# Hybrid decoder trunk on one core: gating chains of the SSD mixer apart and longer, banks of transposed attention weights held longer, the queries' second copy on GpSimd, three longer delays

## The chip, the core and the metric

The kernel runs on one core of a Trainium2 chip. The core has a matrix engine (TensorE, PE in the profile, with its weight loads as PEld), a vector engine (VectorE, DVE), an activation engine (ScalarE, ACT), a general engine (GpSimd, POOL) and a queue that issues most transfers (SyncE, SP). The metric is the device time of one execution in microseconds (us). The kernel before took 1032.54 us (median of 3 runs, 1031.77 to 1033.56).

## The reference

Two layers, each with one RMSNorm, one shared input projection, four parallel mixers and one shared output projection; then a last RMSNorm. Sequence 512, width 1024, all in fp32.

```python
for l in range(DEPTH):                                   # DEPTH = 2
    u = rmsnorm(h, norm_w[l])
    proj = einsum('bsd,de->bse', u, w_in[l])
    ret_p, diff_p, ssd_p, ml_p = split_cols(proj, ...)
    ret_out  = retention_mixer(rq, rk, rv, cos, sin) * silu(rz)
    diff_out = diff_attention_mixer(dq, dk, dv, lam, lam_init, ...) * silu(dz)
    y = ssd_mixer(xbc, dt_raw, ...)
    ssd_out  = _rms(y * silu(sz)) * ssd_norm_w[l]        # one rms over all 512 columns
    ml_out   = mlstm_mixer(mqk, mv, mo, mg, ...) * silu(mz)
    mix = concatenate([ret_out, diff_out, ssd_out, ml_out])
    h = h + einsum('bse,ed->bsd', mix, w_out[l])
return rmsnorm(h, final_norm_w)
```

Differential attention, per block of 128 queries and per head, subtracts two softmaxes:

```python
s = einsum('bqhtd,bkhtd->bhtqk', qi, k)                  # t = 0, 1: two score maps
p = softmax(where(mask, s, NEG_INF))
a = p[:, :, 0] - lam * p[:, :, 1]
out = einsum('bhqk,bkhe->bqhe', a, v)                    # then _rms and norm_w
```

## The kernel before

**Precision.** Each fp32 product is made of three matmuls: weights and activations are split into a high part (cast to fp32r, `whi`, `uh`, `mh`) and the rest (`wlo`, `ul`, `ml`), and hi*hi, hi*lo and lo*hi are summed in one bank. A weight piece comes by a transfer into a buffer `raw` (two of them, 128 x 1024 each, line 370), ACT casts its halves to `whi` (L361), DVE subtracts to get `wlo` (L362); ten buffers of each.

**Tiling.** The 512 positions are four blocks t of 128; a projection of 512 columns is a tile `pspj` of one bank of the matrix engine's accumulator, 24 matmuls of 128x512. There are eight banks. `psum` takes a bank off a heap ordered by the time at which it was put back, `free(p, lag)` puts it back with the modelled time plus `lag`. So `lag` does not wait for anything; it decides which bank the next tile takes. The real wait is a semaphore: the first matmul into a bank waits for the last read of what was there before.

**Order.** Only TensorE's order is written by hand. A planner runs the program in Python with a modelled TensorE clock `clk`. `filler` yields one projection after another in the order of the table `ORDER` (mLSTM's parts, then attention's dk, dq, dv, dz, output projection m, SSD's xs, bc, output projection d, rqk, sz, rv, rz, s, r); each of the four mixers is a generator that is put in by `spawn` and says by `yield x` how many us of matmuls are to stand before its next step. The table `W` has these delays: `dQ` from the split of a head's queries to its scores, `sB` from an SSD chunk's scores to its output, `mB3` the same in mLSTM's last chunk, `sF` from the reduction of a gated SSD chunk to the 128x1 matmul that sums its squares. Other engines' orders follow from the order of issue and a scheduler's priorities; each engine runs its own list in order.

**Places that the change touches.**
- `fin_s` (L1048 to 1076), once per SSD chunk t, after `silu(sz)` is there: gate on GpSimd (L1057), squares and cast on ACT, `ml` on DVE (L1063), the reduction of the squares on DVE into a buffer `bt` (L1065; two buffers), then a delay `sF`, a matmul 128x1 with ones, `m` on DVE (L1070), the power -0.5 on GpSimd. All four chains begin at the same time, when the last `sz` is there.
- `split_q` (L1158 to 1168), once per head: ACT copies each half of 64 rows of the queries to its own rows (L1164) and to the other rows (L1167), DVE makes the low part `ql` (L1165).
- `diff` (L1185 on): scores `psS` into two banks, mask, maximum and exponential (L1206 to 1208, high priority), mix of the two maps (L1215). `diff_av` (L1222 to 1240): transposes of the weights into a bank (L130), its copy to `w` on DVE (L1231, even t) or ACT (L1229, odd t), then the products with v into `psacc`.
- `layer`: in layer 0 the parameters' set-up `params2` is spawned after the first projection.

Of the kernel before, what the change touches and what calls it, by code (L numbers as in the profile page):

```python
# [56 lines left out]
END = {"cv", "cvh", "nlam", "aneg", "fac"}  # L57


W = {'norm': 9.0, 'g1': 1.5, 'g2': 7.3, 'g3': 1.8, 'g4': 12.4, 'mB': 1.8, 'mB3': 3.0, 'mC': 1.3, 'mN': 5.0, 'mF': 9.6, 'sB': 10.2,  # L60
     'sN': 0.0, 'sF': 6.0, 'rC': 2.3, 'rN': 3.0, 'dT': 9.14, 'dN': 1.0, 'dM': 3.0, 'dV': 6.68, 'dF': 14.0,
     'm0': 6.4, 's0': 8.8, 'dT1': 0.6, 'dN1': 1.0, 'he': 100, 'hr': 50, 'hd': 50, 'dS': 4.7, 'dQ': 6.0,
     'ha': 50}


# [31 lines left out]
class Trunk:  # L97
# [228 lines left out]
    def norm_in_t(self, t):  # L326
# [5 lines left out]
        for half in range(2):  # L332
# [3 lines left out]
            us.append(u)  # L336
        yield W["norm"]
        for half in range(2):
# [276 lines left out]
    def ev_conv(self, dst, which, f0, last=None):  # L615
        nc = self.nc

        def f(j, p):
            w = self.cvh[:, which, f0 + j, :]
            acc = self.ev()  # L620
            with self.tc.high_priority(W["he"]):
                if j == last:
# [14 lines left out]
    def ev_rope(self, sink, scale=1.0):  # L637
# [3 lines left out]
        def f(j, p):  # L641
            x = self.ev()
            with self.tc.high_priority(W["hr"]):
                for q in range(4):
# [73 lines left out]
    def gates(self):  # L718
# [11 lines left out]
        self.free(p)  # L730
        yield W["g1"]
        pt = self.psum()
# [22 lines left out]
        for i in range(7, 0, -1):  # L755
# [7 lines left out]
                                op=ALU.mult)  # L763
        yield W["g2"]
        pc = self.psum()
# [28 lines left out]
        nc.vector.tensor_copy(out=st[:, :, 64:68], in_=tot[:, :, 8:12])  # L794
        yield W["g3"]
        pr = self.psum()
# [253 lines left out]
    def fin_s(self, t, y, zs, res, l, fac):  # L1050


        nc = self.nc
        yield from self.pause(("sz", l, 3))
        for j in range(4):
            js = slice(j * P, (j + 1) * P)
            nc.gpsimd.tensor_tensor(out=y[:, js], in0=y[:, js], in1=zs[j][:, t * P:(t + 1) * P], op=ALU.mult)  # L1057
        sq = self.ev()
        nc.scalar.activation(sq, y, AF.Square)
        mh = self.t("mh", [P, 512], F32R, bufs=4)  # L1060
        ml = self.t("ml", [P, 512], F32R, bufs=4)
        nc.scalar.copy(out=mh, in_=y)
        nc.vector.tensor_tensor(out=ml, in0=y, in1=mh.bitcast(F32), op=ALU.subtract)  # L1063
        s = self.t("bt", [P, 256], bufs=2)
        nc.vector.tensor_reduce(out=s[:, 0:P], in_=sq.rearrange("p (j t) -> p t j", j=4), axis=AX.X, op=ALU.add)  # L1065
        yield W["sF"]
        p = self.psum()
        self.mm(p[:, 0:1], lhsT=s[:, 0:P], rhs=self.ones[:, 0:1])
        m = self.sm([P, 1])
        nc.vector.tensor_scalar(m, p[:, 0:1], 0.25 / GW, EPS, ALU.mult, ALU.add)  # L1070
        self.free(p)
        self.rsqrt(fac[:, t:t + 1], m, 1)
        res.append((mh, ml))
        self.done.add(("s", l, t))
# [83 lines left out]
    def split_q(self, x):  # L1158

        nc = self.nc  # L1160
        hi = [self.t("qs", [P, 512], F32R, bufs=2) for _ in range(2)]
        for j in range(2):
            own, oth = slice(j * 64, j * 64 + 64), slice(64 - j * 64, 128 - j * 64)
            nc.scalar.copy(out=hi[j][own, :], in_=x[own, :])  # L1164
            nc.vector.tensor_tensor(out=self.ql[j][own, :], in0=x[own, :], in1=hi[j][own, :].bitcast(F32),  # L1165
                                    op=ALU.subtract)
            nc.scalar.copy(out=hi[j][oth, :], in_=x[own, :])  # L1167
        return hi

    def split_k(self, dst):  # L1170
# [51 lines left out]
    def diff_av(self, l, t, h, a, o, v):  # L1222
        nc = self.nc
        n = (t + 1) * P
        pa = self.tr4([a[:, j * P:(j + 1) * P] for j in range(t + 1)])
        at = self.pg()
        with self.tc.high_priority(W["ha"]):
            if t % 2:
                nc.scalar.copy(out=at[:, 0:n], in_=pa[:, 0:n])  # L1229
            else:  # L1230
                nc.vector.tensor_copy(out=at[:, 0:n], in_=pa[:, 0:n])  # L1231
        self.free(pa)
        yield W["dV"]
        yield from self.pause(("dv", l, t))
        hs = slice(h * P, (h + 1) * P)
        for j in range(t + 1):
            self.mm(o[:, t * P:n], lhsT=at[:, j * P:(j + 1) * P], rhs=v[j][:, hs], start=(j == 0), stop=(j == t))
        self.done.add(("av", l, t, h))
# [43 lines left out]
    def layer(self, l, last):  # L1282

        nc = self.nc
        mv, th, mq, mk, mz, rm = [], [], [], [], [], []
        dv, dz, dq, dk, rd = [], [], [], [], []
        xs, bc, sz, rs = [], [], [], []
        qk, rv, rz, rr = [], [], [], []
        first = [True]
        fac = self.sm([P, NT], tag="fac", bufs=2)  # L1290

        def begin():
            if l:
                yield from self.proj_tok("mv", self.ev_vaug(mv))
            else:
                yield from self.start(self.ev_vaug(mv))
                self.spawn(self.params2(0))

        def mixer(gen, delay=0.0):
            def f():  # L1300
                self.spawn(gen(), delay)
                return ()
            return f

        def got_q(h, x):
            dq.append(x)
            self.done.add(("dq", l, h))

        def after(t):
            if last:  # L1310
                return self.final_t(t)
            if first[0]:
                first[0] = False
                self.params(l + 1)
                self.norm_in()
            return self.norm_in_t(t)

        def end():
            if last:
                self.load_nw(DEPTH, nc.scalar)  # L1320
            yield from self.out_proj("r", rr, True, after, last)

        tok = lambda name, evac: lambda: self.proj_tok(name, evac)
        feat = lambda name, evac: lambda: self.proj_feat(name, evac)
        return {

            "mv": begin,
            "gates": mixer(self.gates),
            "mq": feat("mq", self.ev_conv(mq, 1, 0)),
            "mk": feat("mk", self.ev_conv(mk, 1, 4)),  # L1330
            "mlstm": mixer(lambda: self.mlstm(mv, th, mz, mq, mk, rm), W["m0"]),
            "mo": tok("mo", self.ev_tanh(th)),
            "mz": tok("mz", self.ev_silu(mz, "z", 8)),
            "m": lambda: self.out_proj("m", rm),

            "dk": feat("dk", self.ev_rope(self.split_k(dk))),
            "dv": tok("dv", self.ev_v(dv)),
            "diff": mixer(lambda: self.diff(dq, dk, dv, dz, rd), W["dS"]),
            "dq": feat("dq", self.ev_rope(got_q, 0.125)),
            "dz": tok("dz", self.ev_silu(dz, "z", 8)),  # L1340
            "d": lambda: self.out_proj("d", rd, heads=True),

            "xs": feat("xs", self.ev_conv(xs, 0, 0)),
            "bc": feat("bc", self.ev_conv(bc, 0, 4, 3)),
            "ssd": mixer(lambda: self.ssd(xs, bc[0:2], bc[2:4], sz, rs, fac), W["s0"]),
            "sz": feat("sz", self.silu_feat(sz)),
            "s": lambda: self.out_proj("s", rs, fac=fac),

            "rqk": feat("rqk", self.ev_rope(lambda j, x: qk.append(x))),
            "rv": tok("rv", self.ev_v(rv)),  # L1350
            "ret": mixer(lambda: self.retention(qk, rv, rz, rr)),
            "rz": tok("rz", self.ev_silu(rz, "z", 8)),
            "r": end,
        }
# [77 lines left out]
```

## Time and profile before

| what | value |
|---|---|
| median of 3 runs | 1032.54 us (1031.77 to 1033.56) |
| the profiled execution | 1032.78 us |
| its span, first to last instruction | 1030.9 us, TensorE's mean granted clock 0.995 |
| TensorE busy | 1010.3 us, 98% of the span |
| VectorE, ScalarE, GpSimd busy | 704.4 us (68%), 496.2 us (48%), 170.0 us (16%) |
| chain that ended last, by engine | PE 86%, DVE 6%, DMA 4%, issue 2%, ACT 1% |

TensorE is busy nearly all the time, so what it does not do for want of data is read from the waits of that engine: the view of waits sums the idle time before its instructions by what ended it. A time line lists instructions with start and duration; where an instruction was late, the idle time and its releaser stand in brackets. Rows with the same line and form that follow one another are put together (x4).

### The profile page before, as it was taken

To read this page: it belongs to the slowest core of one execution; us is meant where nothing else is said; L and a number is where in the kernel's file an instruction comes from. 1 tells how busy PE (TensorE), PEld (TensorE's weight loads), DVE (VectorE), ACT (ScalarE), POOL (GpSimd) and SP (SyncE) were. 2 spreads that over 40 slices of the span, in tenths; PEclk is the share of its full clock that TensorE was granted. 3 is DMA by queue.
4 is the path that set the end of the run, shared out by engine and by line. 5 is a ranking of instruction groups with operands and counts; after the bars stand their busy time and mean duration, and the time that the engine had idled before them with its cause. 6 is when DMAs were issued, how large, how long until landed. Compare 5 with 4: busy or idle time off the path is not lost.

```text
span 1030.9 us, 14248 instructions
## 1 busy us (share of the span) xinstructions
PE 1010.3 (98%) x5096; PEld 831.6 (81%) x5096; DVE 704.4 (68%) x1532; ACT 496.2 (48%) x1077; POOL 170.0 (16%) x227
## 2 busy tenths in 40 slices
PE   9999999999999999899999999999999999989997
PEld 6788888788888887778887888887888888878786
DVE  5587676568887866446555967667687787863464
ACT  5445337656565344324353443576564553643332
POOL 1000132201111143122000012211011102421301
PEclk9999999999999999999999999999999999999999
DMA  7333322222212333214122432323141233242112
GB/s 257 109 89 107 103 72 86 85 95 82 82 51 93 106 86 102 75 63 128 42 82 83 132 94 73 92 82 103 62 123 42 82 100 105 86 119 82 41 62 82
DMA packets 39145, 93.84 MB, mean 91 GB/s; under 512 B 3849, under 2 KB 16777, under 8 KB 38946
## 3 DMA queue, kind: packets, MB, share of 16 engines
q1 hardware_dynamic: 38064, 91.48, 28.9%
q10 hardware_dynamic: 1010, 1.45, 0.5%
q8 instruction: 40, 0.66, 0.3%
q14 instruction: 31, 0.25, 0.1%
HBM read 90.77 MB, written 2.15 MB: 90 GB/s over the span
## 4 chain that ended last, share of the span: by engine, by line
PE 86%; DVE 6%; DMA 4%; issue 2%; ACT 1%; POOL 0%; SPq 0%; POOLq 0%; DVEq 0%; ACTq 0%
PE pspj L126 72%; PE psS L126 6%; PE psacc L126 5%; PE psS L130 3%; DMA raw<-in_w_in_dram 2%; DMA w<-in_rows_dram 1%; DVE wlo L362 1%; DMA z<-in_w_in_dram 1%; ACT whi L361 1%; DVE bt L1065 1%; DVE h L699 1%; DVE wlo L365 0%; DVE z L1366 0%; DVE w L992 0%; DVE ml L1063 0%
## 5 line engine op out<-in xcount | busy, mean ns | idle before, releaser
L362 DVE TENSOR_TENSOR wlo<-raw,whi 128x512 fp32r<-128x512 f32 x248 | 173.9, 722 | 77.8 <-ACT whi L361 74.4
L361 ACT CAST whi<-raw 128x512 fp32r<-128x512 f32 x248 | 147.6, 619 | 129.3 <-PE pspj L126 67.7
L126 PE MATMUL pspj<-uh,whi 128*128 128x512 f32 x512 | 203.9, 398 | 1.3 <-DVE w L1231 1.3
L126 PE MATMUL pspj<-uh,wlo 128*128 128x512 f32 x512 | 199.7, 390 | 0.0
L126 PE MATMUL pspj<-ul,whi 128*128 128x512 f32 x512 | 199.5, 390 | 0.0
L126 PE MATMUL pspj<-whi,uh 128*128 128x512 f32 x448 | 183.5, 410 | 0.9 <-ACT whi L361 0.7
L126 PE MATMUL pspj<-whi,ul 128*128 128x512 f32 x448 | 176.9, 395 | 0.2 <-DVE ul L353 0.2
L126 PE MATMUL pspj<-wlo,uh 128*128 128x512 f32 x448 | 172.9, 395 | 0.0
L126 PEld LDWEIGHTS pspj<-uh,whi 128*128 128x128 f32 x512 | 96.2, 188 | 21.3 <-DVE w L1231 2.2
L126 PEld LDWEIGHTS pspj<-uh,wlo 128*128 128x128 f32 x512 | 96.1, 188 | 20.7
L126 PEld LDWEIGHTS pspj<-ul,whi 128*128 128x128 f32 x512 | 96.3, 188 | 18.6
L126 PE MATMUL pspj<-whi,mh 128*128 128x512 f32 (+1 forms) x260 | 104.0, 400 | 2.0 <-DVE w L1231 2.0
L126 PEld LDWEIGHTS pspj<-whi,uh 128*128 128x128 f32 x448 | 85.5, 191 | 19.5 <-ACT whi L361 1.6
L126 PEld LDWEIGHTS pspj<-wlo,uh 128*128 128x128 f32 x448 | 84.8, 190 | 20.4 <-DVE wlo L362 1.4
L126 PE MATMUL pspj<-whi,ml 128*128 128x512 f32 (+1 forms) x260 | 100.8, 388 | 0.3 <-DVE ml L667 0.2
L126 PE MATMUL pspj<-wlo,mh 128*128 128x512 f32 (+1 forms) x260 | 100.7, 387 | 0.0
L126 PEld LDWEIGHTS pspj<-whi,ul 128*128 128x128 f32 x448 | 85.6, 191 | 16.4 <-DVE ul L353 1.0
L243 POOL TENSOR_TENSOR s<-s,nhalf 128x4 f32<-128x4 f32 (+1 forms) x36 | 31.4, 871 | 364.8 <-DVE s L1255 191.0
L628 DVE SCALAR_TENSOR_TENSOR e<-pspj,cvh,e 128x511 f32<-128x511 f32 (+2 forms) x90 | 66.9, 744 | 8.4 <-ACT e L626 7.4
L646 ACT ACTIVATE e<-pspj 32x512 f32<-32x512 f32 x96 | 56.7, 590 | 12.5 <-PE pspj L126 11.2
L126 PEld LDWEIGHTS pspj<-whi,mh 128*128 128x128 f32 x260 | 48.9, 188 | 11.9 <-DVE w L1231 2.8
L126 PEld LDWEIGHTS pspj<-wlo,mh 128*128 128x128 f32 x260 | 48.8, 188 | 10.4
(228 smaller groups left out, 1449.4 us busy)
## 6 DMA issues: line engine op xcount, KB each, us to landing
raw<-in_w_in_dram SPq DMA_DIRECT2D x116, 512.0 KB, 3.9
raw<-in_w_out_dram SPq DMA_DIRECT2D x32, 512.0 KB, 3.4
bcm<-adr SPq DMA_DIRECT2D x16, 256.0 KB, 3.6
z<-in_w_in_dram SPq DMA_DIRECT2D x8, 256.0 KB, 6.9
bcm<-gdr SPq DMA_DIRECT2D x8, 256.0 KB, 3.7
out_dram<-z SPq DMA_DIRECT2D x7, 256.0 KB, 2.0
h<-in_x_dram SPq DMA_DIRECT2D x3, 512.0 KB, 7.4
cst<-in_consts_dram SPq DMA_DIRECT2D x1, 1035.0 KB
```

The costliest lines, as they stand in the source:

```text
L126: self.nc.tensor.matmul(out, lhsT=lhsT, rhs=rhs, start=start, stop=stop, **kw)
L130: self.nc.tensor.transpose(out, src, self.ident if ident is None else ident)
L243: self.nc.gpsimd.tensor_tensor(out=out, in0=m, in1=self.nhalf[:, :n], op=ALU.pow)
L361: nc.scalar.copy(out=hi, in_=raw)
L362: nc.vector.tensor_tensor(out=lo, in0=raw, in1=hi.bitcast(F32), op=ALU.subtract)
L628: nc.vector.scalar_tensor_tensor(acc[:, s:], p[:, 0:S - s], w[:, 3 - s:4 - s], acc[:, s:], ALU.mult, ALU.add)
L646: nc.scalar.activation(x[q * 32:q * 32 + 32, :], p[o * 32:o * 32 + 32, :], AF.Copy, scale=scale)
L699: nc.vector.tensor_tensor(out=hs, in0=p, in1=hs, op=ALU.add)
L1065: nc.vector.tensor_reduce(out=s[:, 0:P], in_=sq.rearrange("p (j t) -> p t j", j=4), axis=AX.X, op=ALU.add)
```

## The change

Seven edits. The table W: `mB3` 3.0 to 4.0, `sB` 10.2 to 12.0, `sF` 6.0 to 14.0, `dQ` 6.0 to 7.0. `fin_s` begins its four chains 3.0 us apart (of the planner's clock). `split_q` makes the second copy of each half on GpSimd in place of ACT. `diff_av` puts the transposes' bank back with a lag of 3.5 in place of 1.0. `params2` of layer 0 is spawned 4.0 later.

```diff
@@ -57,9 +57,9 @@
 END = {"cv", "cvh", "nlam", "aneg", "fac"}
 
 
-W = {'norm': 9.0, 'g1': 1.5, 'g2': 7.3, 'g3': 1.8, 'g4': 12.4, 'mB': 1.8, 'mB3': 3.0, 'mC': 1.3, 'mN': 5.0, 'mF': 9.6, 'sB': 10.2,
-     'sN': 0.0, 'sF': 6.0, 'rC': 2.3, 'rN': 3.0, 'dT': 9.14, 'dN': 1.0, 'dM': 3.0, 'dV': 6.68, 'dF': 14.0,
-     'm0': 6.4, 's0': 8.8, 'dT1': 0.6, 'dN1': 1.0, 'he': 100, 'hr': 50, 'hd': 50, 'dS': 4.7, 'dQ': 6.0,
+W = {'norm': 9.0, 'g1': 1.5, 'g2': 7.3, 'g3': 1.8, 'g4': 12.4, 'mB': 1.8, 'mB3': 4.0, 'mC': 1.3, 'mN': 5.0, 'mF': 9.6, 'sB': 12.0,
+     'sN': 0.0, 'sF': 14.0, 'rC': 2.3, 'rN': 3.0, 'dT': 9.14, 'dN': 1.0, 'dM': 3.0, 'dV': 6.68, 'dF': 14.0,
+     'm0': 6.4, 's0': 8.8, 'dT1': 0.6, 'dN1': 1.0, 'he': 100, 'hr': 50, 'hd': 50, 'dS': 4.7, 'dQ': 7.0,
      'ha': 50}
 
 
@@ -1052,6 +1052,7 @@
 
         nc = self.nc
         yield from self.pause(("sz", l, 3))
+        yield 3.0 * t
         for j in range(4):
             js = slice(j * P, (j + 1) * P)
             nc.gpsimd.tensor_tensor(out=y[:, js], in0=y[:, js], in1=zs[j][:, t * P:(t + 1) * P], op=ALU.mult)
@@ -1164,7 +1165,7 @@
             nc.scalar.copy(out=hi[j][own, :], in_=x[own, :])
             nc.vector.tensor_tensor(out=self.ql[j][own, :], in0=x[own, :], in1=hi[j][own, :].bitcast(F32),
                                     op=ALU.subtract)
-            nc.scalar.copy(out=hi[j][oth, :], in_=x[own, :])
+            nc.gpsimd.tensor_copy(out=hi[j][oth, :], in_=x[own, :])
         return hi
 
     def split_k(self, dst):
@@ -1229,7 +1230,7 @@
                 nc.scalar.copy(out=at[:, 0:n], in_=pa[:, 0:n])
             else:
                 nc.vector.tensor_copy(out=at[:, 0:n], in_=pa[:, 0:n])
-        self.free(pa)
+        self.free(pa, lag=3.5)
         yield W["dV"]
         yield from self.pause(("dv", l, t))
         hs = slice(h * P, (h + 1) * P)
@@ -1294,7 +1295,7 @@
                 yield from self.proj_tok("mv", self.ev_vaug(mv))
             else:
                 yield from self.start(self.ev_vaug(mv))
-                self.spawn(self.params2(0))
+                self.spawn(self.params2(0), 4.0)
 
         def mixer(gen, delay=0.0):
             def f():
```

(In the kernel after, lines from 1055 on stand one lower.) Three places of the new order follow; `psS` and `psacc` are tiles of banks, `uh` and `ul` the normalised input, `bt` the reduced squares of an SSD chunk.

TensorE in layer 0, the four 128x1 matmuls of the SSD's gating, before:

```order
L126 MATMUL pspj_4110<-whi_4086,ul_76 128x512
L126 MATMUL pspj_4110<-wlo_4087,uh_75 128x512
L126 MATMUL psS_4193<-ones,bt_4124 128x1
L126 MATMUL psS_4198<-ones,bt_4136 128x1
L126 MATMUL psS_4203<-ones,bt_4148 128x1
L126 MATMUL psS_4208<-ones,bt_4160 128x1
L126 MATMUL pspj_4174<-whi_4044,uh_75 128x512
L126 MATMUL pspj_4174<-whi_4044,ul_76 128x512
L126 MATMUL pspj_4174<-wlo_4045,uh_75 128x512
```

and after:

```order
L126 MATMUL pspj_4189<-whi_4070,ul_76 128x512
L126 MATMUL pspj_4189<-wlo_4071,uh_75 128x512
L126 MATMUL psS_4235<-ones,bt_4124 128x1
L126 MATMUL pspj_4228<-whi_3857,uh_75 128x512
L126 MATMUL pspj_4228<-whi_3857,ul_76 128x512
...
L126 MATMUL pspj_4228<-whi_4044,ul_76 128x512
L126 MATMUL pspj_4228<-wlo_4045,uh_75 128x512
L126 MATMUL psS_4277<-ones,bt_4152 128x1
L126 MATMUL pspj_4228<-whi_4066,uh_75 128x512
...
L126 MATMUL pspj_4316<-wlo_4250,uh_75 128x512
L126 MATMUL psS_4348<-ones,bt_4209 128x1
L126 MATMUL pspj_4316<-whi_4269,uh_75 128x512
```

The four stood in a row; now 15 matmuls of 128x512 stand between the first and the second, 15 and the retention's first scores and transposes between the second and the third, and 9 between the third and the fourth.

TensorE in layer 0 at head 1's first two blocks of scores, from the last matmul of the `dz` tile of block t=1 (`pspj_2232`, read by ACT L577 and DVE L579), before:

```order
L126 MATMUL pspj_2232<-wlo_2186,uh_75 128x512
L126 MATMUL pspj_2285<-whi_2107,uh_75 128x512
L126 MATMUL pspj_2285<-whi_2107,ul_76 128x512
L126 MATMUL pspj_2285<-wlo_2108,uh_75 128x512
L126 MATMUL pspj_2285<-whi_2146,uh_75 128x512
L126 MATMUL pspj_2285<-whi_2146,ul_76 128x512
L126 MATMUL pspj_2285<-wlo_2147,uh_75 128x512
L126 MATMUL psS_2361<-ft_1680,qs_2248 128x384
L126 MATMUL psS_2361<-ft_1680,ql_448 128x384
L126 MATMUL psS_2362<-ft_1681,qs_2249 128x384
L126 MATMUL psS_2362<-ft_1681,ql_450 128x384
L126 MATMUL psacc_2039<-v_2015,w_2283 128x128
```

and after:

```order
L126 MATMUL pspj_2232<-wlo_2167,uh_75 128x512
L126 MATMUL pspj_2278<-whi_2107,uh_75 128x512
L126 MATMUL pspj_2278<-whi_2107,ul_76 128x512
L126 MATMUL pspj_2278<-wlo_2108,uh_75 128x512
L126 MATMUL psS_2339<-ft_1680,qs_2251 128x256
L126 MATMUL psS_2339<-ft_1680,ql_448 128x256
L126 MATMUL psS_2340<-ft_1681,qs_2252 128x256
L126 MATMUL psS_2340<-ft_1681,ql_450 128x256
L126 MATMUL pspj_2278<-whi_2146,uh_75 128x512
L126 MATMUL pspj_2278<-whi_2146,ul_76 128x512
L126 MATMUL pspj_2278<-wlo_2147,uh_75 128x512
L126 MATMUL pspj_2358<-whi_1955,uh_75 128x512
```

After the change the tile of block t=3, `pspj_2358`, is put into the bank that `pspj_2232` had, ten matmuls behind its end; before, no tile of a projection is put there so soon, and t=3's tile begins later, in another bank. On DVE the reader of the bank, L579, stands behind the mix of head 1's first block (L1215 in the kernel before) and the second block's masks.

ScalarE in layer 0, head 3's blocks of 384 and 512 columns (`w` from `psS`), before:

```order
L1208 ACTIVATE w_2938,rsum_2870<-psS_2940,s_924_2937 128x384
L631 ACTIVATE e_2930<-e_2925 128x512
L1208 ACTIVATE w_2939,rsum_2870<-psS_2941,s_924_2937 128x384
L1249 ACTIVATE e_2961,s_932_2960<-psacc_2577 128x128 x4
L626 ACTIVATE e_3026<-pspj_2862,cvh_457 128x512
L1208 ACTIVATE w_2995,rsum_2870<-psS_2997,s_940_2994 128x512
L1208 ACTIVATE w_2996,rsum_2870<-psS_2998,s_940_2994 128x512
L1229 COPY w_3041<-psS_3038 128x256
L361 CAST whi_3058<-raw_3056 128x512
```

and after:

```order
L626 ACTIVATE e_3003<-pspj_2844,cvh_474 128x512
L361 CAST whi_3053<-raw_3051 128x512
L1209 ACTIVATE w_2979,rsum_2897<-psS_2981,s_930_2978 128x384
L1209 ACTIVATE w_2980,rsum_2897<-psS_2982,s_930_2978 128x384
L631 ACTIVATE e_3008<-e_3003 128x512
L1209 ACTIVATE w_3023,rsum_2897<-psS_3025,s_942_3022 128x512
L361 CAST whi_3057<-raw_3051 128x512
L1209 ACTIVATE w_3024,rsum_2897<-psS_3026,s_942_3022 128x512
```

A cast of weights, `whi_3053`, has come to stand ahead of the two exponentials of the 384 columns. It takes the buffer of `whi_2494`, whose last reader on TensorE stands just ahead of head 3's scores of 512 columns, with one matmul between.

## Rows read from the trace of the kernel before

**Rows 1.** The page's first part: busy time, share of the span, instructions of each engine.

```profile
PE 1010.3 (98%) x5096; PEld 831.6 (81%) x5096; DVE 704.4 (68%) x1532; ACT 496.2 (48%) x1077; POOL 170.0 (16%) x227
```

**Rows 2.** Waits of TensorE: what waited, its releaser, us in total, times, longest.

```profile
PE psS L126 <- DVE bt L1065: 5.2, 3, 2.3
PE pspj L126 <- DVE w L1231: 3.2, 4, 1.0
...
PE pspj L126 <- ACT whi L361: 0.7, 2, 0.4
PE psacc L126 <- DVE w L996: 0.7, 1, 0.7
PE psacc L126 <- DVE w L890: 0.7, 2, 0.3
PE psS L126 <- DVE s L1070: 0.5, 1, 0.5
```

**Rows 3.** Time line of TensorE, 268 to 274 us: start, duration, instruction [idle before].

```profile
271.13 0.39 PE L126 MATMUL pspj<-wlo,mh 128*128 128x512 f32 x1
272.50 0.50 PE L126 MATMUL pspj<-whi,mh 128*128 128x512 f32 x1 [0.98 <-DVE w L1231]
272.83 0.40 PE L126 MATMUL pspj<-whi,ml 128*128 128x512 f32 x1
```

**Rows 4.** Time line of TensorE at the SSD's gating, layer 0.

```profile
419.09 0.50 PE L126 MATMUL psS<-ones,bt 128*128 128x1 f32 x4
421.88 0.38 PE L126 MATMUL psS<-ones,bt 128*128 128x1 f32 x2 [2.29 <-DVE bt L1065]
```

**Rows 5.** Time line of VectorE at the same place.

```profile
420.82 1.93 DVE L1065 TENSOR_REDUCE bt<-e 128x128 f32<-128x512 f32 x2
```

**Rows 6.** Stretches behind it in both layers: busy time by engine, PEclk, DMA, GB/s.

```profile
423.00:426.00 3.00, 3.00 (x9) 2.42 (x10) 0.16 (x1) 0.00 (x0) 2.02 (x4) 0.50 0.00 0
...
928.50:931.30 2.80, 2.80 (x8) 2.22 (x9) 0.16 (x1) 0.00 (x0) 1.80 (x4) 0.50 0.00 0
```

**Rows 7.** Time line of ScalarE, 184 to 199 us.

```profile
185.97 0.62 ACT L1167 CAST qs<-ft 64x512 fp32r<-64x512 f32 x1
...
197.26 1.14 ACT L361 CAST whi<-raw 128x512 fp32r<-128x512 f32 x2 [2.24 <-DMA raw<-in_w_in_dram]
```

**Rows 8.** Time line of TensorE at head 1's first scores.

```profile
230.20 0.28 PE L126 MATMUL psS<-ft,qs 128*128 128x256 f32 x1
```

**Rows 9.** Time line of VectorE at the same place.

```profile
233.42 0.29 DVE L1206 TENSOR_TENSOR psS<-psS,cst 128x128 f32<-128x128 f32 x1
...
234.78 0.69 DVE L579 SCALAR_TENSOR_TENSOR z<-e,pspj 128x512 f32<-128x512 f32 x1 [0.61 <-ACT e L577]
```

**Rows 10.** Time line of ScalarE, 290 to 302 us.

```profile
291.08 0.58 ACT L1208 ACTIVATE w<-psS,s 128x384 f32<-128x384 f32 x1
...
294.77 0.78 ACT L626 ACTIVATE e<-pspj,cvh 128x512 f32<-128x512 f32 x1 [1.98 <-PE pspj L126]
```

**Rows 11.** Time line of VectorE, 290 to 300 us.

```profile
297.62 0.75 DVE L628 SCALAR_TENSOR_TENSOR e<-pspj,cvh,e 128x509 f32<-128x509 f32 x1
```

**Rows 12.** Time line of VectorE and TensorE at the SSD's first chunk, layer 0.

```profile
337.37 0.68 DVE L633 SCALAR_TENSOR_TENSOR ft<-e,e 128x512 f32<-128x512 f32 x1
...
340.84 0.39 PE L126 MATMUL psS<-ft,ft 128*128 128x128 f32 x2
```

**Rows 13.** Groups of GpSimd: busy us, mean ns, idle before.

```profile
L649 POOL TENSOR_TENSOR e<-e,cst 128x512 f32<-128x512 f32 x24 | 31.2, 1301 | 109.0 <-ACT e L646 109.0
```

**Rows 14.** Time line of VectorE, 190 to 198 us.

```profile
190.95 1.24 DVE L362 TENSOR_TENSOR wlo<-raw,whi 128x512 fp32r<-128x512 f32 x1
...
197.91 0.69 DVE L362 TENSOR_TENSOR wlo<-raw,whi 128x512 fp32r<-128x512 f32 x1 [1.01 <-ACT whi L361]
```

**Rows 15.** Time line of ScalarE, then TensorE: head 2's last copy, its first scores.

```profile
245.92 0.62 ACT L1167 CAST qs<-ft 64x512 fp32r<-64x512 f32 x1
...
255.31 0.36 PE L126 MATMUL psS<-ft,qs 128*128 128x256 f32 x1
```

## The prediction, made before the result was known

> **What bounds the kernel now.** I read the page's first part first: TensorE is busy 1010.3 us [rows 1] of a span of 1030.9, so an edit that leaves the matmuls as they are can give back only what TensorE waits. The view of waits of TensorE says for what [rows 2]: the reduced squares of the SSD's gating (5.2 and 0.5 us), copies of transposed attention weights (3.2), casts of weights (0.7), the SSD's weights in its last chunk (0.7), mLSTM's in its last chunk (0.7). Idle time of the other engines counts only where it ends in one of these.
>
> What a wait costs is more than its row. In the time line the matmul at 271.13 is followed at 272.50 and that one at 272.83, where undisturbed ones stand 0.23 apart [rows 3]: 1.14 late and 0.10 more at the restart, 1.24 in all where the row says 0.98 idle. So I take a wait of the view at its idle time plus 0.26.
>
> **The change part by part.** The profiled execution took 1032.78 us, 1.9 outside its span, which nothing here touches, and 0.24 above the median. No matmul is added or taken away; the sum is one of waits.
>
> *SSD's gating (`sF` 14, chains 3 us apart).* Before, four 128x1 matmuls begin at 419.09 and two of them are late by 2.29 [rows 4], because the reductions have two buffers: the third and fourth run at 420.82 to 422.75 [rows 5], after the first matmuls have read theirs. Behind the pause the granted clock is 0.50 for 3.0 us in layer 0 and for 2.8 in layer 1 [rows 6]: half of 2.4 GHz, so half of this time is lost, 1.5 and 1.4. With the view's 5.2 + 0.5 this makes 5.7 + 2.9 = 8.6 us for two layers. After, 15, 15 and 9 matmuls of 0.23 us stand between the four, 3.4, 3.4 and 2.0 us. A reduction takes about 0.97 (1.93 for two, rows 5), and the buffer of the first is free 6.8 us before the third is wanted. I take the whole 8.6. If DVE reaches the third reduction early, it stands in DVE's list waiting for the first matmul with weights' subtractions behind it; half of the gain would go. What this leaves is 4.3 to 8.6.
>
> *Banks held longer (lag 3.5).* The four waits for L1231 cost 3.2 + 4 x 0.26 = 4.2 us. After, the next tile is put into another bank; I followed the eight banks through the new order, and no later user of a transposes' bank comes sooner than 6.5 us of matmuls after the transposes. Gain 4.2, with a bound of zero if the banks were taken as before.
>
> *Queries' second copy on GpSimd.* On ACT two copies of 0.62 leave the row in front of the ropes and casts at 185 to 198 us [rows 7], so the chain behind (ropes, casts, the subtractions that free a `raw` buffer, the transfer for which the cast at 197.26 waits 2.24) comes 1.24 earlier. TensorE's two waits for that cast cost 0.7 + 2 x 0.26 = 1.2; 1.24 a layer covers the 0.6 of each. Gain 1.2. The copies themselves take on GpSimd something between 0.62 (ACT's) and 1.30, a 128x512 operation with two inputs [rows 13]; I take 1.0, nearer to the row of the same engine. They are hidden in front of head 2, the tightest place I found in GpSimd's list: its last copy ended at 246.54, its first scores began at 255.31 [rows 15], 8.8 us later.
>
> What GpSimd does beside DVE has a price in the trace: with a rope product running, a subtraction of `wlo` took 1.24, without it 0.69 [rows 14]. Sixteen copies could each stretch one or two such subtractions by 0.55. At head 0 they fall on DVE's idle time in front of the rope (ACT's row is the releaser there), so I take nothing, and up to 0.55 a head, 4.4 us, as the end of the range. The Trainium skill (GPSIMD Engine Reference, 8. Key points) states that GpSimd shares its SBUF interfaces with VectorE and that DVE instructions with two SBUF inputs contend; the trace's 1.24 against 0.69 agrees. The same page (4.1 Engine selection) calls one-input work on GpSimd roughly line-rate; by this a copy would take about 0.7, an estimate from DVE's 0.69, and the sum would stay as it is, since the copies are hidden either way.
>
> *Delays `mB3` and `sB`.* 4.0 for 3.0 puts three more matmuls and four transposes, 1.1 us, ahead of mLSTM's last products; the two waits there cost 0.7 + 0.52 = 1.2 and are covered. `sB` puts nine more matmuls, 2.0 us, ahead of the SSD's output, where the wait costs 0.7 + 0.26 = 1.0: covered. Gain 2.2.
>
> *`dQ` 7 and `params2`.* Head by head the scores come 1 us later in TensorE's order, four heads 4 us. This by itself costs nothing, but it moves the end of head 3 against the output projection. At the start DVE's order is the same row for row, so I count nothing for `params2`.
>
> Gains: 8.6 + 4.2 + 1.2 + 2.2 = 16.2.
>
> **What is late next.** Before shows no wait at these places; they come from the new order with before's durations, a layer each.
> 1. `dz`'s tile of block t=3 takes the bank of t=1's, whose reader L579 now stands behind head 1's masks. In the trace the first scores begin at 230.20 [rows 8], the second block's second mask runs at 233.42 and takes 0.29, and L579 0.69 [rows 9], so the bank is free at about 234.35, 4.15 after the first scores. In the new order the tile comes two score blocks (0.47 each) and nine matmuls (0.23) behind them, 3.0: a wait of 1.15 plus 0.1, 1.25.
> 2. The cast ahead of head 3's exponentials: 0.57 (half of 1.14, rows 7) and two exponentials of 0.58 [rows 10] end 1.73 after the cast's release, the handover some 0.2 more; TensorE needs both banks 1.14 (five matmuls) after it. 0.8 and 0.1: 0.9.
> 3. A convolution's bank is taken 3.4 after its last matmul; from ACT's 294.77 [rows 10] to the end of DVE's 298.37 [rows 11] it needed 3.6: 0.2 and 0.1, 0.3.
> 4. The SSD's first scores come 15 matmuls, 3.4 us, sooner behind head 3; DVE's L633 ended at 338.05 and they ran at 340.84 [rows 12], 2.8 to spare: 0.6 and 0.1, 0.7.
> Together 3.15, 6.3 for two layers. Each is bounded below by zero, if the engine gets to it earlier than in the trace of before, and above by about twice: on GpSimd's side, DVE rows stretched.
>
> Sum: 1032.78 - 16.2 + 6.3 = 1022.9; against the median, 0.24 less, 1022.6 us.
>
> **The rivals.**
> - *No new wait bites*: DVE and ACT run ahead of the trace at these four places. 1032.5 - 16.2 = 1016.3. For it: ACT is freed of 16 copies, 10 us. Against: the four places hang on order, not on load. Chance 0.15.
> - *The gains are halved at the gating or the new waits are twice as long*: 1022.6 + 4.3 = 1026.9, or 1022.6 + 6.3 = 1028.9. For it: DVE is the engine that all four share, and GpSimd's copies stretch it. Against: the distances in the new order are 2 to 3.4 us where the work is 1. Chance 0.27.
> - *Slower: the lag takes more than it gives.* Thirty-two sets of transposes hold a bank 2.5 us of the planner's clock longer, so that projections, scores and convolutions get banks that were freed later, and wait for DVE and ACT. I count 6.3/32 = 0.2 us for each set. At (16.2 + 2)/32 = 0.57 the kernel is slower by more than 0.2%; at 0.6 it takes 1032.5 - 16.2 + 19.2 = 1035.5. For it: the dearest wait of this kind in before costs 1.24 [rows 3]. Against: I find two to three such places a layer, not sixteen. Chance 0.06.
> - *It doesn't do what it says*: the chains of the gating still meet at two buffers and the banks come out alike, so that only the new waits and the small gains remain, 1032.5 - 3.4 + 6.3 = 1035, or nothing. The new order speaks against both. Chance 0.02.
>
> **How the numbers follow.** The forecast has 0.50, its own range 1019 to 1026. The range for 8 in 10 reaches from all gains without a new wait, 1015.5 (with a rounded 0.8 for short gaps that the view leaves out), to the doubled new waits, 1029.5. What a measurement can tell from no change is 0.2%, 2.1 us. Faster by more: 0.50 + 0.15 + most of 0.27 = 0.89; within: 0.05; slower: 0.06.
>
> **What would show it.** Right: in the view of waits of TensorE the rows for `bt` and for L1231 are gone, no stretch of 0.50 clock stands behind the gating, the cast at 197 us is not waited for; new rows name L579 (about 1 us each layer) and ACT's exponential. Wrong: a row for `bt` stays; the new rows add up to more than 8 us or are absent; rows of `psS` from `qs` wait for GpSimd.

## The result, and the profile after

The changed kernel takes 1019.66 us (median of 4 runs, 1019.34 to 1019.92), the kernel before 1032.44 beside it; the ratio is 0.9875, with a 95% interval of 0.9858 to 0.9892. The forecast was 1022.6 in a range of 1015.5 to 1029.5: the time lies inside, 2.9 us under the forecast. Time went down by 12.8 us where 9.9 were forecast.

The page's first part of the kernel after, then its view of waits of TensorE (what waited, its releaser, us in total, times, longest; rows of the start and of 0.3 us and less left out):

```profile
span 1017.8 us, 14268 instructions
...
PE 1005.0 (99%) x5096; PEld 828.2 (81%) x5096; DVE 698.9 (69%) x1532; ACT 483.9 (48%) x1061; POOL 189.8 (19%) x243
```

```profile
PE pspj L126 <- DVE z L579: 1.9, 2, 1.0
PE psS L126 <- ACT w L1209: 1.2, 2, 0.6
...
PE psS L126 <- DVE ft L633: 0.4, 2, 0.2
```

All six rows of [rows 2] are gone. In their place stand the three new waits that the new order had foretold, twice each, once a layer: `dz`'s bank behind L579, the exponential of 384 columns behind a cast, the SSD's first scores behind L633. The convolution's bank has no row. Of the 13.1 us by which the span is shorter, 7.8 are idle time of TensorE and 5.3 its busy time (1005.0 for 1010.3), of which the half clock of [rows 6] makes 2.9.

The largest of them in the time line of TensorE, layer 0: the `dz` tile of t=3 after the second block of scores.

```profile
230.10 0.27 PE L126 MATMUL psS<-ft,qs 128*128 128x256 f32 x1
...
232.88 0.39 PE L126 MATMUL pspj<-wlo,uh 128*128 128x512 f32 x1
234.24 0.50 PE L126 MATMUL pspj<-whi,uh 128*128 128x512 f32 x1 [0.97 <-DVE z L579]
234.58 0.39 PE L126 MATMUL pspj<-whi,ul 128*128 128x512 f32 x1
```

1.36 instead of 0.23 at the wait and 0.34 instead of 0.23 behind it: 1.24 us, where the working from [rows 8, 9] gave 1.25. The second, in the time line of ScalarE and then of TensorE: the cast holds the exponentials up, and the second map's scores of 512 columns wait for the bank of the first of them (ACT's last read of it ends at 294.70, while the second exponential runs on).

```profile
293.51 0.62 ACT L361 CAST whi<-raw 128x512 fp32r<-128x512 f32 x1 [1.04 <-PE pspj L126]
294.03 0.57 ACT L1209 ACTIVATE w<-psS,s 128x384 f32<-128x384 f32 x1
294.51 0.19 ACT L1209 ACTIVATION_READ_ACCUMULATOR w<-psS,s 128x1 f32 x1
294.60 0.57 ACT L1209 ACTIVATE w<-psS,s 128x384 f32<-128x384 f32 x1
```

```profile
293.08 0.39 PE L126 MATMUL pspj<-ul,whi 128*128 128x512 f32 x1
...
293.76 0.39 PE L126 MATMUL psS<-ft,ql 128*128 128x512 f32 x1
294.75 0.50 PE L126 MATMUL psS<-ft,qs 128*128 128x512 f32 x1 [0.60 <-ACT w L1209]
295.09 0.40 PE L126 MATMUL psS<-ft,ql 128*128 128x512 f32 x1
```

0.99 instead of 0.23 and 0.34 instead of 0.23: 0.87, where 0.9 was forecast. L633's wait costs some 0.45 a layer (0.2 idle and 0.26), the convolution's nothing: 2.56 a layer, 5.1 in all, where 6.3 was forecast.

At the gating TensorE does not stop; DVE waits for it, for 0.35 us. Its time line in the kernel after (the reduction is L1066 there):

```profile
424.64 0.69 DVE L362 TENSOR_TENSOR wlo<-raw,whi 128x512 fp32r<-128x512 f32 x1 [6.27 <-ACT whi L361]
425.25 1.08 DVE L1066 TENSOR_REDUCE bt<-e 128x128 f32<-128x512 f32 x1
...
428.65 1.08 DVE L1066 TENSOR_REDUCE bt<-e 128x128 f32<-128x512 f32 x1 [0.35 <-PE psS L126]
```

The third and fourth reductions run 1.08 each behind the first and second matmuls, but the matmuls that need them come 5 us and more later (432.99 and 435.30 in TensorE's time line), and the granted clock stays whole there (columns: stretch, its length, busy time and count of PE, PEld, DVE, ACT, POOL, then PEclk, DMA share, GB/s; compare [rows 6]):

```profile
424.00:434.00 10.00, 10.00 (x54) 8.12 (x53) 7.24 (x14) 4.58 (x8) 1.49 (x2) 1.00 0.36 111
```

### The profile page after: what moved, and what is told of

Its sections match the earlier page's. It is cut to its first block, busy times and chain, and to the rows that moved or that the text cites. A ratio compares the mean times of both kernels' runs of the same rounds, so it can differ in the third digit from the quotient of the medians.

```text
span 1017.8 us, 14268 instructions
## 1 busy us (share of the span) xinstructions
PE 1005.0 (99%) x5096; PEld 828.2 (81%) x5096; DVE 698.9 (69%) x1532; ACT 483.9 (48%) x1061; POOL 189.8 (19%) x243
## 4 chain that ended last, share of the span: by engine, by line
PE 92%; DVE 3%; ACT 2%; DMA 1%; issue 1%; SPq 1%; POOL 0%; POOLq 0%; ACTq 0%; DVEq 0%
PE pspj L126 77%; PE psS L126 6%; PE psacc L126 5%; PE psS L130 3%; DVE e L628 1%; DMA z<-in_w_in_dram 1%; DVE h L699 1%; DVE z L1367 0%; DVE wlo L362 0%; DMA raw<-in_w_in_dram 0%; ACT e L256 0%; SPq L453 0%; DMA raw<-in_w_out_dram 0%; ACT e L626 0%; DVE ft L633 0%
## 5 line engine op out<-in xcount | busy, mean ns | idle before, releaser
L362 DVE TENSOR_TENSOR wlo<-raw,whi 128x512 fp32r<-128x512 f32 x248 | 171.4, 714 | 63.8 <-ACT whi L361 60.8
L126 PEld LDWEIGHTS pspj<-whi,ul 128*128 128x128 f32 x448 | 84.5, 189 | 16.2 <-DVE ul L353 1.4
L126 PEld LDWEIGHTS pspj<-whi,ml 128*128 128x128 f32 x260 | 49.0, 188 | 9.7 <-DVE ml L667 1.1
```

Of the source, the lines that this page charges most:

```text
L126: self.nc.tensor.matmul(out, lhsT=lhsT, rhs=rhs, start=start, stop=stop, **kw)
L362: nc.vector.tensor_tensor(out=lo, in0=raw, in1=hi.bitcast(F32), op=ALU.subtract)
```

## The experiments

Twelve kernels ran, in three sets, each set on one chip; each is given with its ratio to runs of the kernel before in its set. None leaves out any of the computation.

**What is the gating worth, and is the rest untouched?** `e1_gate`, before with these two edits (of the table W only the entry is shown, here and below):

```diff
-'sF': 6.0
+'sF': 14.0
     yield from self.pause(("sz", l, 3))
+    yield 3.0 * t
```

> The kernel before with the gating's two edits alone (sF 14, chains 3 us apart). Theory (the waits are independent and add up): the rows for bt and the half-clock stretches behind them go in both layers, everything else stays, 8.6 us less than before, about 1023.8. Rival (what is won at the gating is lost at the output projection s, which now gets its factors later): half or less, 1028 or more, with new waits of pspj in the last fifth of each layer.

Measured: 1023.61 us, ratio 0.9901 (0.9886 to 0.9916). The rows for `bt` are gone, and no half clock follows the gating; of the rest only L996's row grew, from 0.7 to 1.6. The first theory holds, with more than its 8.6 us: 9.9 less than before in its set (8.7 to 11.8 by the interval), two thirds or more of the whole gain. The rival's new waits in the last fifth of a layer are not there.

**Are the two buffers the cause of the pause?** `e2_gate_buf`, before with the reduction written into the chain's own `w` tile:

```diff
-s = self.t("bt", [P, 256], bufs=2)
+s = y
```

> The kernel before, with the four reductions written into the four w tiles that are free by then, in place of two bt buffers; delays as before. Theory A (as predicted: two buffers make the third and fourth chain late): the pause goes, about 8 us less than before, 1024. Theory B (DVE's own work of four subtractions and four reductions, 6.6 us in a row, is what is late, and the buffers only set its order): the pause stays within 1 us a layer, 1030 to 1033.

Measured: 1035.49 us, ratio 1.0021 (1.0010 to 1.0031): a little slower. Its waits of TensorE:

```profile
PE psS L126 <- DVE w L1065: 6.6, 6, 1.5
```

The matmuls now wait one by one for a DVE that is busy without a break from 415.9 to 423.7 (its time line; columns as above):

```profile
417.84 1.09 DVE L1065 TENSOR_REDUCE w<-e 128x128 f32<-128x512 f32 x1
418.86 1.27 DVE L1063 TENSOR_TENSOR ml<-w,mh 128x512 fp32r<-128x512 f32 x2
420.06 1.94 DVE L1065 TENSOR_REDUCE w<-e 128x128 f32<-128x512 f32 x2
421.93 0.67 DVE L1063 TENSOR_TENSOR ml<-w,mh 128x512 fp32r<-128x512 f32 x1
```

Theory A's 1024 is missed by 11 us; the time lies above theory B's 1030 to 1033 too, since here each reduction must also wait until `ml` has read the tile that it overwrites (the first runs at 417.84, in before at 415.18). That DVE's own work is late is to be seen without this run, in the time line of DVE of before:

```profile
419.02 1.88 DVE L1063 TENSOR_TENSOR ml<-w,mh 128x512 fp32r<-128x512 f32 x3
```

It ends at 420.90, where the third reduction begins [rows 5]: DVE had no idle time in front of it, though the first 128x1 matmul had begun at 419.09. So the prediction's reason for the pause, "because the reductions have two buffers", is not sufficient. Four `bt` buffers without the tie to `ml`, which could let DVE reduce first, were not run.

**Then is it the time?** `e5_gate_delay` has sF 14 alone, `e12_delay_own_buffers` sF 14 and `s = y`; `e6_gate_apart` has `yield 3.0 * t` alone.

> The kernel before with sF 14 alone: the four 128x1 matmuls stand 36 matmuls of TensorE (8 us) later, but again in a row. Theory A (what counts is that a third reduction can't begin before the first matmul has read its buffer): two reductions of 1 us follow the first two matmuls while TensorE has nothing else, so 2 us of pause and 1.4 of half clock a layer stay: 1031 to 1033. Theory B (DVE is late with its own work, and 8 us more cover it): the pause goes, about 1024.

Measured: 1028.79 us, ratio 0.9949 (0.9930 to 0.9967): some half of the gain of `e6_gate_apart` in the same set (10.2), between the theories and within neither's range. The time line of TensorE shows the two reductions that theory A named, with a shorter pause than in [rows 4]:

```profile
427.66 0.50 PE L126 MATMUL psS<-ones,bt 128*128 128x1 f32 x4
429.28 0.38 PE L126 MATMUL psS<-ones,bt 128*128 128x1 f32 x2 [1.12 <-DVE bt L1065]
430.20 0.38 PE L126 MATMUL psS<-ones,bt 128*128 128x1 f32 x2 [0.54 <-DVE bt L1065]
```

(Each 128x1 matmul leaves two records, so x4 are the first two of the four matmuls, and each x2 is one. On DVE the third reduction, at 428.22, also stands behind a subtraction of weights; since the matmul at 427.66 had to read the buffer first, that is worth less than 0.6 us.)

> The kernel before with sF 14 and the four reductions written into the four free w tiles: 8 us later, in a row, each with a buffer of its own. Theory A (the pause has two causes in series, DVE's work up to 422 us and then the two buffers): with both out of the way no pause, about 1024. Theory B (DVE begins the reductions only when TensorE has come to the matmuls): as with the delay alone, 1028.8.

Measured: 1023.47 us, ratio 0.9899 (0.9880 to 0.9918); all eight records of the four matmuls stand in one row, without a wait, and the next matmul follows at once:

```profile
428.19 0.95 PE L126 MATMUL psS<-ones,w 128*128 128x1 f32 x8
428.99 0.49 PE L126 MATMUL pspj<-whi,uh 128*128 128x512 f32 x1
```

Theory A holds. So the pause had two causes, one behind the other: DVE's own work, and behind it the two buffers. Own buffers alone leave the first, 8 us more alone leave the second.

> The kernel before with the chains 3 us apart alone, sF 6: 15, 15 and 12 matmuls stand between the four, the first where it stood before. Theory A: the third reduction begins 3.4 us before its matmul, so the pause goes, about 8 us less, 1024 to 1025. Theory B (DVE's work of 6.6 us in front of the first two): the second matmul still waits 1 to 2 us, 1026 to 1029.

Measured: 1024.07 us, ratio 0.9905 (0.9890 to 0.9920), with no row for `bt`. Theory A holds. Spacing alone does what both edits do: DVE runs the third reduction at 421.27, behind the first matmul (419.48), and the matmul that needs it comes at 426.77; the fourth runs at 423.44, behind the second matmul (423.13), for a matmul at 429.74. The longer sF adds nothing that can be measured (1024.07 against 1023.61, in two sets).

**Does the lag remove the waits for the copies of transposed weights?** `e3_lag_back`, after with

```diff
-self.free(pa, lag=3.5)
+self.free(pa)
```

> The kernel after with the transposes' lag back at 1.0. Theory A (as predicted: the lag removes the four waits for L1231): they come back, 4.2 us more than after, about 1023.9. Theory B (read from the new order: with dQ 7 the bank windows at those places are long whatever the lag): no row for L1231, the same as after within 1 us, 1019 to 1020.5.

Measured: 1020.39 us, ratio 0.9870 (0.9855 to 0.9885), the kernel after's within its interval. No row for the copy, and the new waits as in the kernel after:

```profile
PE pspj L126 <- DVE z L579: 1.9, 2, 1.0
PE psS L126 <- ACT w L1209: 1.2, 2, 0.6
```

Theory B's time holds, against the prediction: beside dQ 7.0 the lag changes no time that can be told. Neither the 4.2 us gained nor the new waits are the lag's. But its reason, long bank windows, holds at one of two places a layer. At head 3 the bank of the first block's transpose is taken 7.3 us behind it, where before took it 4.6 behind. At head 2 the window is as short as before, and DVE's copy comes sooner; the transpose, the copy and the next tile in that bank (the banks are read from the program, not from the profile), in before and then in `e3_lag_back`:

```profile
266.20 0.27 PE L130 MATMUL psS<-cst,w 128*128 128x128 f32 x1
...
272.16 0.28 DVE L1231 COPY w<-psS 128x128 f32<-128x128 f32 x1
```

```profile
267.73 0.27 PE L130 MATMUL psS<-cst,w 128*128 128x128 f32 x1
...
272.65 0.28 DVE L1232 COPY w<-psS 128x128 f32<-128x128 f32 x1
...
272.99 0.50 PE L126 MATMUL pspj<-uh,whi 128*128 128x512 f32 x1
```

In before the copy ended 6.2 us behind the transpose, and the tile at 272.50 waited for it [rows 3]; here it ended 5.2 behind it and the tile begins 5.3 behind it, 0.1 late.

**Then they are dQ's?** `e4_dQ6`, after with `'dQ': 6.0`.

> The kernel after with dQ back at 6.0. Theory A (the new waits for L579, the exponential of 384 columns and L633 come from the later scores): all three kinds go, 5.1 us less than after; one bank at head 3 is then taken 1.58 us behind a convolution's tile, and the exponential of 512 columns in front of it costs some 0.7 a layer, so 1019.7 - 5.1 + 1.4 = 1016.0. Theory B (they come from the lag): they stay, about 1019.7 or more.

Measured: 1015.91 us, ratio 0.9827 (0.9812 to 0.9841), below the kernel after's interval. The longest wait of TensorE behind the start:

```profile
PE pspj L126 <- ACT w L1209: 0.6, 1, 0.6
```

All three new waits are gone, in both layers. Theory A holds; its sum is met within 0.1 us with some luck, since the wait for the exponential of 512 columns came in layer 0 alone. The later scores cost 4.5 us (against `e3_lag_back` in the same set) and buy what the lag buys by itself. `e9_dQ6_lag_back` is this kernel with the lag at 1.0:

> The kernel after with dQ 6.0 and the transposes' lag back at 1.0. Theory A (at dQ 6.0, and only there, the lag keeps two tiles a layer out of the transposes' banks): the four waits for the copy w come back, 4.2 us, and cover the 0.8 for the exponential, so 1015.9 + 3.4 = 1019.3. Theory B (the lag does nothing at either dQ): 1015.9.

Measured: 1019.98 us, ratio 0.9867 (0.9849 to 0.9884), and the row is back:

```profile
PE pspj L126 <- DVE w L1232: 3.7, 4, 1.2
```

Theory A holds: at dQ 6.0 the lag is worth some 4 us (1019.98 against 1015.81 in the same set for the lag of 2.5, below). The two edits are two ways to the same gain, and only dQ's has a price.

**The copies on GpSimd.** `e10_dQ6_q_back` is `e4_dQ6` with the copies on ACT:

```diff
-nc.gpsimd.tensor_copy(out=hi[j][oth, :], in_=x[own, :])
+nc.scalar.copy(out=hi[j][oth, :], in_=x[own, :])
```

> The kernel after with dQ 6.0 and the queries' second copies back on ACT. Theory A (the copies on ACT delay the cast at 197 us): TensorE's two waits for the cast come back with the small gaps around them, 1.2 to 2.0 us more than with the copies on GpSimd, 1017.1 to 1017.9. Theory B (the later orders cover it): 1015.9.

Measured: 1018.20 us, ratio 0.9845 (0.9827 to 0.9863), 2.4 us above the kernel with lag 2.5 of the same set. The row is back and longer than the 0.7 of [rows 2]:

```profile
PE pspj L126 <- ACT whi L361: 1.1, 2, 0.6
```

Theory A holds; the worth is above its 1.2 to 2.0 and twice the prediction's 1.2. In the time line of TensorE:

```profile
196.56 0.40 PE L126 MATMUL pspj<-wlo,uh 128*128 128x512 f32 x1
197.52 0.50 PE L126 MATMUL pspj<-whi,uh 128*128 128x512 f32 x1 [0.56 <-ACT whi L361]
197.86 0.40 PE L126 MATMUL pspj<-whi,ul 128*128 128x512 f32 x1
198.25 0.50 PE L126 MATMUL pspj<-wlo,uh 128*128 128x512 f32 x1
198.58 0.40 PE L126 MATMUL pspj<-whi,uh 128*128 128x512 f32 x1
```

0.96, 0.34, 0.39 and 0.33 where undisturbed matmuls stand 0.23 apart: 1.1 us for one wait, 0.56 of it in the row. `e4_dQ6`, whose matmuls have the same order, has nothing of this there.

**Is there a delay with no short bank?** `e7_dQ61` (dQ 6.1), `e8_dQ575` (dQ 5.75) and `e11_dQ6_lag25` (dQ 6.0, lag 2.5) were meant to beat `e4_dQ6`.

> The kernel after with dQ 6.1. In its order no bank is taken within 1.8 us of its last reader's release, neither behind dz, the convolutions nor the exponentials. If the waits left in the runs before are all of this kind, only mix's 0.4 a layer at the output projection d stays: 0.87 a layer less than with 6.0, about 1014.2. If such small steps only move the waits about: 1015 to 1017.

> The kernel after with dQ 5.75. One short bank is left, 1.36 us behind a DVE update of h with the low part of a mix (0.69) in front of the release: 0.2 to 0.6 a layer; the mix at the output projection d has 0.7 us more than with 6.1 and is not waited for. About 1014.5; the rival as in the run with 6.1.

> The kernel after with dQ 6.0 and the lag at 2.5. In its order the short bank behind head 3 goes to the tile of the first exponential of 512 columns, which ends 0.69 before the second, so the wait of 0.76 that the run with lag 3.5 has in layer 0 goes: 1015.1. Rival: another bank is short, 1015.9 or more.

Measured: 1016.37 (0.9832, 0.9817 to 0.9847), 1016.67 (0.9833, 0.9818 to 0.9848) and 1015.81 (0.9826, 0.9809 to 0.9844). All three miss, by 0.7 to 2.2 us, and the rival of each is nearer: a bank is still short. One row of the time line of TensorE for each, in this order:

```profile
287.32 0.45 PE L126 MATMUL psS<-ft,qs 128*128 128x384 f32 x1 [0.93 <-ACT w L1209]
```

```profile
266.21 0.41 PE L130 MATMUL psS<-cst,w 128*128 128x128 f32 x2 [1.34 <-DVE ml L667]
```

```profile
766.74 0.50 PE L126 MATMUL pspj<-whi,mh 128*128 128x512 f32 x1 [0.55 <-ACT w L1209]
```

The second had been put at 0.2 to 0.6; the first and third had not been seen at all from distances in the order: I followed the causes at these three places no further. The kernels with dQ 6.0, `e4_dQ6` and `e11_dQ6_lag25`, have the lowest medians, but they ran in other sets than these two, and the intervals of all four ratios overlap: no difference between the four can be told.

## Why the prediction was right, and where it was not

**The bound, and the way to count.** TensorE's waits explain the gain: 13.1 us of span against six rows that went and three that came, with the slow clock behind the gating. A wait at its idle time plus 0.26 held (0.97 idle cost 1.24, 0.60 cost 0.87), but not everywhere: the short gaps around a wait can double it, as at the cast.

**The gating, 8.6 us.** Somewhat under: `e1_gate` won 8.7 to 11.8 us, the medians 9.9 apart. The prediction left its own 0.26 for a restart out of these waits. In before the rest of the four matmuls is

```profile
422.81 0.58 PE L126 MATMUL psS<-ones,bt 128*128 128x1 f32 x2 [0.55 <-DVE bt L1065]
423.25 0.77 PE L126 MATMUL pspj<-whi,uh 128*128 128x512 f32 x1
```

so from 419.09 to the next projection 4.16 us passed (4.23 in layer 1), where `e12_delay_own_buffers` needs 0.80: 3.4 a layer, 6.8 in two, where 5.7 was taken; with the 2.9 of slow clock 9.7. (The 2.29 late is the third matmul, the fourth is 0.55 later still; "two of them late by 2.29" misread the records.) The reason was half: two buffers, and in front of them DVE's work (`e2_gate_buf`, `e5_gate_delay`, `e12_delay_own_buffers`). That DVE would stand in its list for the first matmul did happen in the kernel after, 0.35 us, with nobody waiting.

**The lag, 4.2 us.** The waits went, but the step failed in its cause: "after, the next tile is put into another bank" is true of the kernel after, but at dQ 7.0 the waits stay away without it too, at one place because the order takes the bank later, at the other because the copy comes 1 us sooner (`e3_lag_back`). The bound of 6.5 us was not right either: one set that ACT copies is followed in its bank after 5.0 us, without a wait. I had followed the banks through the whole changed order and then credited one of the edits. For the sum it made no difference; for whoever would undo an edit it does.

**The copies, 1.2 us.** Mis-sized: worth some 2.4 at dQ 6.0 (`e10_dQ6_q_back`; its five runs lie 1.1 to 3.2 above those of `e11_dQ6_lag25`), 2.1 of it at the two casts. The view of waits leaves out the short gaps around a wait. GpSimd's copies took 0.60 to 1.12, median 0.72, where 1.0 was taken; the 0.7 that followed from the Trainium skill (GPSIMD Engine Reference, 4.1 Engine selection) was nearer. Of DVE's sixteen subtractions that make `ql` four ran beside such a copy: two took 0.68, two 0.99, where 0.69 was the longest in before; the copies beside them took 1.12, the least disturbed 0.60. That agrees with the contention that the Trainium skill (GPSIMD Engine Reference, 8. Key points) speaks of. No wait of TensorE names these rows.

**`mB3` and `sB`, 2.2 us.** Both rows are gone in the kernel after. L890's is there in each of the five runs without these edits, L996's in four of them; no run has the two edits alone.

**`params2`, nothing.** The start depends on when a transfer lands, not on this edit. DVE's L309, which waits for it, ran at 22.07 us in the profile of before, at 21.38 after, and at 21.13 in `e5_gate_delay`, which has the old delay. So 0.7 us or so of the transfer's time is no effect. On TensorE 0.4 of it is left: its 251st record began at 61.5 us in before and 61.1 in the kernel after, and between 60.5 and 62.0 in all fourteen profiles, whichever delay they have.

**The new waits, 6.3 us.** Places right for three of four, sizes 1.24, 0.87, 0.45 and 0 for 1.25, 0.9, 0.7 and 0.3. They come from dQ alone (`e4_dQ6`). The first is right in its working: the bank was free 4.14 us behind the first scores for 4.15, and wanted 3.0 behind them. The second is right in size by luck: it counted both exponentials, 0.58 too much, but TensorE waited only for the first one's bank; and it put the handover to the cast at 0.2 and the scores 1.14 behind the cast's release, where the cast began 0.43 and the scores fell due 0.91 behind the start of the releasing matmul (293.08). The slower rival, thirty-two held banks at 0.57 each, is refuted in its mechanism: the lag has no price that can be told at either dQ.

**The sum.** Forecast 16.2 of gains less 6.3; measured 12.8, and with 5.1 of new waits 17.9 of gains. The errors that the runs show are 1.2 of new waits put too high, 1.2 of the copies and 1.1 of the gating put too low: together 3.5, a little more than the 2.9 that were missed. What is left of it lies in the terms that no run has alone and in the start, and stays open. The range's upper end was said to be the doubled new waits; these make 1028.9, not 1029.5.

## What to carry to other kernels

Where one engine is nearly full, list its waits, take each with its restart, and read from the new order how far every reader stands from its next writer: that gave each of three new waits within 0.25 us, one of them by luck. But credit a gain to an edit only after undoing that edit: two edits here buy the same 4 us, and leaving out the one with a side effect gains 4.5 us more. A pause with two causes in series shows no gain when only the inner one is removed (two buffers made four), so try the combination before dropping either.

## What the runs showed of the hardware

The fall of the granted clock does not follow a pause's length alone. In the kernel before, 2.29 us idle and 0.55 more (the row at 422.81, above) were followed by 0.50 for 3.0 us [rows 4, 6]. With four own buffers (`e2_gate_buf`) three pauses of 1.47, 0.64 and 1.21 stood close together; in layer 0 they were followed by 0.50 for 3 us (424 to 427 us), and in layer 1, with the same three pauses, for 6 us:

```profile
929.50:935.50 6.00, 6.00 (x16) 4.74 (x17) 0.16 (x1) 0.00 (x0) 1.03 (x2) 0.50 0.00 0
```

With the delay alone (`e5_gate_delay`), 1.12 and 0.54 of idle time were followed by a fall too, in layer 1 to 0.51 over 3.4 us (936.0 to 939.4). A single pause of 1.34 us, with dQ 5.75, was not; the stretch with the pause and the one behind it:

```profile
264.40:266.40 2.00, 0.66 (x6) 0.25 (x4) 1.97 (x6) 0.00 (x0) 0.75 (x1) 1.00 0.00 0
266.40:270.00 3.60, 3.60 (x18) 2.98 (x17) 3.50 (x9) 1.71 (x5) 1.97 (x5) 1.00 0.00 0
```

So what a pause costs behind its end lay between nothing and 3 us (half of 6.0) in these runs. It also differs between executions of one kernel: those of before had a mean granted clock of 0.996 to 0.992 and took 1031.5 to 1036.6 us, the longest at the lowest clock; the kernels without the pause at the gating had 0.997 to 0.999, and the four or five executions of each lie within 1.8 us.
